# Input stage of a hybrid attention block: all eight token tiles first, or the first four and then the projections

## The chip, the cores and the metric

The kernel runs on one core of a Trainium2 chip. The metric is device time in microseconds (us): the median of three runs is 789.06 us (788.49 to 789.99). The profile is of one execution.

Engines: PE (TensorE, matmuls), DVE (VectorE), ACT (ScalarE), POOL (GpSimd), SP (SyncE, which issues most DMAs).

## The reference, cut to what matters

One decoder layer: an adaLN-modulated RMSNorm of `x`, one combined input projection, two attention groups, and an output projection with a residual and a final norm. All shapes are 1024 tokens by 1024 features, float32. The change touches only the first lines:

```python
mod = jax.nn.silu(c) @ ada_w[l] + ada_b[l]             # ada_w: 1024 x 3072
shift, scl, gate = jnp.split(mod, 3, axis=-1)
h = rms_norm(x, norm_g[l]) * (1.0 + scl[:, None, :]) + shift[:, None, :]
proj = h @ w_in[l]                                      # 1024 x 2744, split into 13 parts
(q_n, kc_n, vc_n, ks_n, vs_n, kw_n, vw_n, ...) = jnp.split(proj, IN_OFFSETS, axis=-1)
```

Everything after the first projections (compression, three sparse branches, latent attention, output) is the same in both kernels.

## The kernel before, in words

Tokens lie in eight tiles of 128 (`x_load(t)`, 512 KB each), features in eight blocks of 128 (index `k`). The input stage makes, for each block `k`, the modulated and transposed activations `h` of all 1024 tokens, split into a high part `hh[k]` and a low part `hl[k]` (both fp32r), and feeds them at once into two projections: `kc` (256 columns, features on the partitions, four PSUM banks `kcT{ci}_{hf}`, where `hf` is the token half) and `ks` (256 columns, tokens on the partitions, of tiles 0 to 3 only, two banks). Each product is three matmuls: high by high, high weight by low weight, low by high (`mm_kc` L315, `mm_ks` L325). All further projections (`pj`, L589) follow once `hh` and `hl` are complete.

A token tile passes `x_stat` (ACT squares and sums it, L351; DVE L164 and a POOL power L165 make its reciprocal norm), `x_turn` (DVE scales it, L356; PE transposes it in eight 128x128 pieces, L362) and `x_put` (ACT L370 and DVE L372 copy it out of PSUM into `xnT`).

A block's modulation needs two columns of `silu(c) @ ada_w`. `ad_load(k)` brings 1 MB in two halves, each of two DMAs. `mod_acc` adds the first six of eight row groups on DVE (L288, L290), the last two go to PE (L284), and `mod_mm` (L297) adds the sum over partitions; for block 0 all eight go to PE. `mod_cols` (DVE L302 to L305) makes scale and bias `ab`, `h_high` (ACT L310, twice) applies them, `h_low` (DVE L313) forms the low part. `w_split` splits the weights of two blocks at a time: ACT rounds (`whi`, L262), POOL subtracts (`wlo`, L263).

The order of the work in this stage is written out by hand for all five engines (`tc.manual_schedule`), so each engine executes its list in program order, and an instruction that waits holds back those behind it. First a loop over the eight tiles, with the modulation of block 0 between them; then a skewed loop over `s_`: in one step PE runs high products of block `s_-2`, the modulation of a later block and low products of block `s_-3`, while ACT and DVE prepare block `s_-1`. `x` tiles and `ada_w` halves share one ring of eight buffers (`big`). The sine and cosine tables (`tables`, DVE L396 to L416) and the copies of `kc` out of PSUM (`kc_evac`, DVE L442, ACT L444) close the stage.

Of the kernel before, what the change touches and what calls it, by code (L numbers as in the profile page):

```python
# [73 lines left out]
MLA_LAG = 3  # L74
MLA_WO = 27
AD_CUT = 2
MOD_CUT = 1
X_AD = 4
MOD_PE = (0,)
MOD_DVE = 6  # L80
MOD_FIRST = 4
TAB0 = 4
ACC0 = {5: ((0, 0, 2),), 6: ((0, 2, 4),), 7: ((0, 4, 6),), 8: ((0, 6, 8),), 9: ((1, 0, 2),)}
ENGS0 = ("PE", "SP", "DVE", "Activation", "Pool")
MLA_MIX = (40, 43)
WRING = 12
# [8 lines left out]
def f32(ap):  # L95
    return ap.bitcast(F32)
# [11 lines left out]
def hybrid_block(ctx, tc, x, c, positions, ada_w, ada_b, norm_g, w_in, cmp_pos, cmp_k_w1, cmp_k_w2,  # L108
# [148 lines left out]
    def w_split(k2, pl, tag, wmax, bufs, dst):  # L257
        raw = raws.pop((tag, k2))
        for j in range(2):
            whi = pl.tile([P, wmax], F32R, name="whi" + tag, tag="whi" + tag, bufs=bufs)  # L260
            wlo = pl.tile([P, wmax], F32R, name="wlo" + tag, tag="wlo" + tag, bufs=bufs)
            nc.scalar.activation(whi[:, :256], raw[:, j, :256], AF.Copy)  # L262
            nc.gpsimd.tensor_tensor(wlo[:, :256], raw[:, j, :256], f32(whi[:, :256]), op=ALU.subtract)  # L263
            dst[2 * k2 + j] = (whi, wlo)

    def ad_load(k):
        ads[k] = []
        for q in range(AD_CUT):
# [3 lines left out]
                nc.sync.dma_start(ad[:, :, j, :], ada_r[:, q * n:(q + 1) * n, o + k * P:o + (k + 1) * P])  # L272
            ads[k].append(ad)

    def mod_acc(k, k0, k1):
        if k0 == 0:
            pas[k] = mx_bank(f"mod{k}")
        first = 0 if k in MOD_PE else MOD_DVE
        n = KD // AD_CUT
        for kk in range(k0, k1):  # L280
            src = ads[k][kk // n][:, kk % n]
            if kk >= first:
                for j in range(2):
                    nc.tensor.matmul(pas[k][:, j:j + 1], src[:, j], sc[:, kk:kk + 1], start=(kk == first and j == 0),  # L284
                                     stop=(kk == KD - 1 and first == 0), skip_group_check=True)
            elif kk == 0:
# [12 lines left out]

    def mod_cols(k):  # L300
        pa = pas.pop(k)
# [145 lines left out]
    with tc.manual_schedule(engines={mybir.EngineType[e] for e in ENGS0}):  # L447
        nc.sync.dma_start(rows[0:8], c.rearrange("o (k p) -> (o k) p", p=P))
        x_load(0)
        small_loads()  # L450
        for t in range(1, X_AD):
            x_load(t)
        ad_load(0)
        for t in range(X_AD, NT):
            x_load(t)
        kc_raw(0)
        ks_raw(0)
        ad_load(1)
# [19 lines left out]
        def skew(k, i0, i1):
            for i in range(i0, i1):
                if k < KD:  # L480
                    mod_acc(k, 4 + i, 5 + i)
                if k + 1 < KD:
                    mod_acc(k + 1, i, i + 1)

        mod_mm(0)
        mod_cols(0)
        h_high(0)
        ks_split(0)
        mod_acc(1, 2, 4)
        for s_ in range(1, KD + 3):  # L490
            if s_ + 1 < KD:
                ad_load(s_ + 1)
            if s_ % 2 == 1 and s_ // 2 + 1 < KD // 2:
                kc_raw(s_ // 2 + 1)
                ks_raw(s_ // 2 + 1)
            if 1 < s_ < KD:
                (kc_split if s_ % 2 else ks_split)(s_ // 2)
            if MOD_FIRST <= s_ <= KD:
                mod_mm(s_ - 1)
            if 0 <= s_ - 2 < KD:  # L500
                mm_kc(s_ - 2, (0, 1))
            skew(s_, 0, MOD_CUT)
            if 1 < s_ <= KD:
                if s_ < MOD_FIRST:
                    mod_mm(s_ - 1)
                mod_cols(s_ - 1)
                h_high(s_ - 1)
            skew(s_, MOD_CUT, 4)
            if 2 < s_ < 6:
                next(post)  # L510
            if s_ == KD - 1:
                tables(TAB0)
            if s_ == KD:
                tables(9)
            if s_ - 1 < KD:
                h_low(s_ - 1)
            if 0 <= s_ - 2 < KD - 1:
                mm_ks(s_ - 2, (0, 1))
            if 0 <= s_ - 3 < KD:
                mm_kc(s_ - 3, (2,))  # L520
                if s_ - 3 == KD - 1:
                    mm_ks(s_ - 3, (0, 1))
                mm_ks(s_ - 3, (2,))
# [1072 lines left out]
```

## Time and profile before

| What | us |
|---|---|
| median of three runs | 789.06 |
| the profiled execution | 788.64 |
| its span (first to last instruction) | 786.9 |
| around the span | 1.74 |
| PE busy over the span | 739.3 |
| DVE busy | 583.6 |
| ACT busy | 396.3 |
| POOL busy | 228.0 |

Times inside the trace count from the start of the span. A matmul's end is modelled, so start-to-start distances say more than its duration. [...] The stage that the change touches is the first tenth of the span, up to the first `pj` matmul.

### The profile page before, as it was taken

How to read it: one execution, taken by the hardware profiler on the slowest of the kernel's cores; microseconds unless marked ns; L12 is line 12 of the kernel's file. 1: busy time of each engine (PE TensorE's matmuls, PEld its weight loads, DVE VectorE, ACT ScalarE, POOL GpSimd, SP SyncE). 2: the span in 40 equal slices, each digit the busy share in tenths (PEclk: the TensorE clock that was granted, in tenths of full speed). 3: DMA queues.
4: the chain of work that ended last, by engine and by line, in shares of the span. 5: the costliest groups of instructions: out<-in, count | busy, mean ns of one | idle time of the engine just before them, and what ended most of it. 6: DMA issues, size and time to landing. Idle time of an engine off the chain costs nothing.

```text
span 786.9 us, 17257 instructions
## 1 busy us (share of the span) xinstructions
PE 739.3 (94%) x6464; PEld 653.9 (83%) x6464; DVE 583.6 (74%) x1549; ACT 396.3 (50%) x697; POOL 228.0 (29%) x287
## 2 busy tenths in 40 slices
PE   4999999999999999997899999999988989999996
PEld 3988998989999999995677887777877777888885
DVE  3688745587688788888898889987888878654433
ACT  5354534133122331217899977987556566632212
POOL 3334433154231143504443312110200040154322
PEclk9599999999999999999999999999999979999999
DMA  8961423242531121103311123013010140435431
GB/s 307 262 197 49 127 55 108 61 121 80 162 95 48 44 52 47 36 31 97 93 47 44 43 56 82 22 57 80 10 28 16 52 151 29 151 131 185 144 113 54
DMA packets 60513, 70.18 MB, mean 89 GB/s; under 512 B 5957, under 2 KB 46728, under 8 KB 60430
## 3 DMA queue, kind: packets, MB, share of 16 engines
q1 hardware_dynamic: 55646, 64.62, 27.8%
q10 hardware_dynamic: 4784, 4.47, 1.7%
q8 instruction: 51, 0.84, 0.4%
q14 instruction: 32, 0.26, 0.1%
HBM read 48.33 MB, written 11.53 MB: 76 GB/s over the span
## 4 chain that ended last, share of the span: by engine, by line
PE 76%; DVE 9%; issue 4%; ACT 4%; DMA 4%; POOL 2%; SPq 1%; POOLq 0%; DVEq 0%; ACTq 0%
PE pj L589 24%; PE out L1528 11%; PE o L937 5%; PE pm L841 4%; PE s L994 3%; PE s L995 3%; PE kcT L321 2%; PE mo L937 2%; PE hid L642 2%; PE kq L1180 2%; PE ms L1301 2%; DVE L L1010 2%; PE ms L1302 2%; PE ms L1303 2%; PE mm L1256 2%
## 5 line engine op out<-in xcount | busy, mean ns | idle before, releaser
L589 PE MATMUL pj<-whi,hh 128*128 128x288 f32 (+2 forms) x544 | 161.4, 297 | 0.0
L589 PE MATMUL pj<-wlo,hh 128*128 128x288 f32 (+2 forms) x544 | 158.6, 292 | 0.0
L589 PE MATMUL pj<-whi,hl 128*128 128x288 f32 (+2 forms) x544 | 157.6, 290 | 0.0
L589 PEld LDWEIGHTS pj<-wlo,hh 128*128 128x128 f32 x544 | 102.5, 189 | 1.4
L589 PEld LDWEIGHTS pj<-whi,hh 128*128 128x128 f32 x544 | 102.5, 189 | 0.4
L589 PEld LDWEIGHTS pj<-whi,hl 128*128 128x128 f32 x544 | 102.2, 188 | 0.0
L1010 DVE TENSOR_TENSOR L<-E,H 128x1024 f16<-128x1024 f32 x74 | 92.0, 1243 | 13.1 <-ACT H L1005 11.4
L799 DVE CUSTOM_DVE_ANT_0 junk<-pm,maskw 128x256 bf16<-128x256 f32 (+3 forms) x160 | 77.7, 486 | 16.4 <-PE pm L841 4.4
L1004 ACT ACTIVATE E<-s 128x1024 f32<-128x1024 f32 x74 | 76.4, 1032 | 19.8 <-PE s L995 12.2
L937 PEld LDWEIGHTS <-H 128*128 128x128 f16 x1184 | 57.2, 97 | 30.2 <-issue 17.5
L968 POOL TENSOR_TENSOR mixn<-mixn,tmp 128x256 f32<-128x256 f32 x32 | 44.8, 1400 | 108.7 <-DVE tmp L967 101.9
L1005 ACT ACTIVATE H<-s 128x1024 f16<-128x1024 f32 x74 | 76.2, 1030 | 0.0
L841 PE MATMUL pm<-ka,qall 128*128 128x448 f32 (+5 forms) x208 | 67.2, 323 | 0.2 <-DVE mp L796 0.2
L937 PE MATMUL o<-v,H 128*128 128x65 f16 (+1 forms) x1056 | 60.0, 195 | 4.6 <-DVE mixn L964 4.6
L211 POOL TENSOR_TENSOR wlo<-wraw,whi 128x288 fp32r<-128x288 f32 (+2 forms) x64 | 51.7, 832 | 31.6 <-ACT whi L210 29.3
L994 PE MATMUL s<-qa,ka 128*128 128x512 f32 x132 | 57.9, 439 | 2.9 <-ACT H L1005 2.5
L937 PE MATMUL o<-v,L 128*128 128x65 f16 x528 | 56.7, 193 | 0.0
L937 PEld LDWEIGHTS <-L 128*128 128x128 f16 x592 | 55.7, 100 | 0.0
L708 ACT ACTIVATE zt<-pj 128x288 f32<-128x288 f32 (+1 forms) x32 | 12.2, 384 | 74.3 <-PE pj L589 62.6
L1314 ACT ACTIVATE lat<-ms 128x1024 f32<-128x1024 f32 (+2 forms) x40 | 32.6, 815 | 31.1 <-PE ms L1303 14.9
L1316 DVE TENSOR_TENSOR mL<-lat,mH 128x1024 f16<-128x1024 f32 (+2 forms) x40 | 39.0, 988 | 9.7 <-ACT mH L1315 9.5
L995 PE MATMUL s<-qall,kb_early 128*128 128x512 f32 x108 | 43.4, 401 | 0.0
(384 smaller groups left out, 1892.1 us busy)
## 6 DMA issues: line engine op xcount, KB each, us to landing
ad<-in_ada_w_dram SPq DMA_DIRECT2D x32, 256.0 KB
wraw<-in_w_in_dram SPq DMA_DIRECT2D x20, 288.0 KB
x<-in_x_dram SPq DMA_DIRECT2D x8, 512.0 KB
gw<-in_ada_w_dram SPq DMA_DIRECT2D x32, 128.0 KB
qa<-qall SPq DMA_DIRECT2D x32, 128.0 KB
wor<-in_w_out_dram SPq DMA_DIRECT2D x16, 256.0 KB
xr<-in_x_dram SPq DMA_DIRECT2D x8, 512.0 KB
out_dram<-y SPq DMA_DIRECT2D x7, 512.0 KB
```

Of the source, the lines that this page charges most:

```text
L211: split.tensor_tensor(wlo[:, :width], raw[:, j, :width], f32(whi[:, :width]), op=ALU.subtract)
L589: nc.tensor.matmul(pt[:, :width], a[k][:, ts], b[:, :width], start=(n == 0), stop=(n == 23))
L799: nc.vector.tensor_tensor_reduce(out=junk[:, :w], in0=scores, in1=mask, scale=1.0, scalar=2.0 * NEG, op0=ALU.add, op1=ALU.max, accum_out=dst)
L841: nc.tensor.matmul(bank[:, :total_w], lhs, keys, start=True, stop=True)
L937: nc.tensor.matmul(po[:, c0:c0 + hi - lo], a[:n, qs], v[:, lo:hi], start=start and j == 0, stop=stop and j == 2, skip_group_check=True)
L968: nc.gpsimd.tensor_tensor(mv, mv, tmp, op=ALU.add)
L994: nc.tensor.matmul(dst, a, staged[u], start=True, stop=False)
L995: nc.tensor.matmul(dst, b, qc[u], start=False, stop=mk is None)
L1004: nc.scalar.activation(Et, pS, AF.Exp, scale=SC_NSA)
L1005: nc.scalar.activation(ph, pS, AF.Exp, scale=SC_NSA)
L1010: nc.vector.tensor_tensor(pl, Et, ph, op=ALU.subtract)
L1528: nc.tensor.matmul(po, a[:, kk], b[hf][k][:, cs.start - hf * 512:cs.stop - hf * 512], start=(n == 0), stop=(n == 23))
```

## The change

The loop over tiles is cut at tile 4. Tiles 0 to 3 are loaded, normed and transposed as before; then a loop over blocks `k` makes modulation, `h` and both projections for the first 512 tokens. Tiles 4 to 7 are normed and transposed inside blocks 1 to 3 (`x_work`). The second token half of `h` and of `kc` (`second`) follows inside blocks 4 to 7 (`SECOND`). Block 0 now also adds six row groups on DVE. `h_high` and `h_low` work on 512 columns at a time, so there are twice as many of them; `tables` is spread over blocks 3 to 7. The loads are issued in the new order of use.

```diff
-ACC0 = {5: ((0, 0, 2),), 6: ((0, 2, 4),), 7: ((0, 4, 6),), 8: ((0, 6, 8),), 9: ((1, 0, 2),)}
+KC_RING = 6
+SECOND = {4: (0, 1), 5: (2, 3), 6: (4,), 7: (5, 6, 7)}
...
-    def h_high(k):
-        hfs[k] = sp.tile([P, S], F32, name=f"hf32_{k}", tag="hf32", bufs=2)
-        for dst in (hh[k], hfs[k]):
-            nc.scalar.activation(dst, xnT[:, k], AF.Identity, scale=ab[:, 0, k:k + 1], bias=ab[:, 1, k:k + 1])
+    def h_high(k, hf):
+        hs = slice(hf * 512, (hf + 1) * 512)
+        hfs[k, hf] = sp.tile([P, 512], F32, name=f"hf32_{k}_{hf}", tag="hf32", bufs=4)
+        for dst in (hh[k][:, hs], hfs[k, hf]):
+            nc.scalar.activation(dst, xnT[:, k, hs], AF.Identity, scale=ab[:, 0, k:k + 1], bias=ab[:, 1, k:k + 1])
...
-        for s_ in range(NT + 2):
-            if s_ < NT:
+        for s_ in range(6):
+            if s_ < 4:
                 x_stat(s_)
...
+        for t in (4, 5):
+            x_load(t)
+        ad_load(2)
+        kc_raw(1)
+        ks_raw(1)
+        kc_split(0)
+        ks_split(0)
+        mod_acc(0, 0, MOD_DVE)
...
+        def second(k, part):
+            if part == 0:
+                h_high(k, 1)
+            else:
+                h_low(k, 1)
+                mm_kc(k, 1, (0, 1, 2))
+
+        x_work = {1: ((x_stat, 4),), 1.5: ((x_turn, 4), (x_stat, 5)), 2: ((x_put, 4), (x_turn, 5), (x_stat, 6)),
+                  2.5: ((x_put, 5), (x_turn, 6), (x_stat, 7)), 3: ((x_put, 6),), 3.5: ((x_turn, 7), (x_put, 7))}
+        late_loads = {0: ((x_load, 6), (x_load, 7)), 1: ((ad_load, 3), (kc_raw, 2), (ks_raw, 2)),
+                      2.5: ((ad_load, 4), (ad_load, 5)), 3: ((kc_raw, 3), (ks_raw, 3)), 3.5: ((ad_load, 6), (ad_load, 7))}
...
+        for k in range(KD):
+            mod_acc(k + 1, 0, 2)
+            mod_mm(k)
+            mod_cols(k)
+            if k:
+                mm_kc(k - 1, 0, (2,))
+                mm_ks(k - 1, (2,))
+            h_high(k, 0)
+            if k % 2 and k < KD - 1:
+                kc_split(k // 2 + 1)
+                ks_split(k // 2 + 1)
+            extra(k)
...
+            mod_acc(k + 1, 2, MOD_DVE)
+            h_low(k, 0)
+            mm_kc(k, 0, (0, 1))
+            mm_ks(k, (0, 1))
...
+            for j in SECOND.get(k, ()):
+                second(j, 1)
+            extra(k + 0.5)
+            if k > 2:
+                tables(1)
```

Two places of the instruction lists matter, one on PE and one on DVE. In these rows the digit behind a name is its block or tile (`mod2` is block 2, `x4` tile 4), the number after the underscore only tells buffers apart.

PE before, between the high products of block 1 and the low products of block 0:

```order
L321 MATMUL kcT1_1_361<-hh1_91,wloa_310 128x512
L297 MATMUL mod2_391<-ones_pp_71,acc2_392 128x1 x2
L284 MATMUL mod3_426<-sc_77,ad3_1_406 128x1 x4
L329 MATMUL ks0_0_362<-whi_374,hh1_91 128x256
L329 MATMUL ks0_0_362<-wlo_375,hh1_91 128x256
```

PE of the changed kernel, from the end of block 1's high products to the start of block 2's:

```order
L323 MATMUL ks0_1_289<-wlo_276,hh1_91 128x256
L356 MATMUL xT4_0_400<-ident_66,x4_249 128x128 x4
L356 MATMUL xT4_1_405<-ident_66,x4_249 128x128 x4
L287 MATMUL mod2_418<-sc_77,ad2_1_256 128x1 x4
L291 MATMUL mod2_418<-ones_pp_71,acc2_327 128x1 x2
L315 MATMUL kcT0_0_286<-hl1_99,whia_267 128x512
L315 MATMUL kcT1_0_287<-hl1_99,whia_267 128x512
L323 MATMUL ks0_0_288<-whi_275,hl1_99 128x256 x2
L323 MATMUL ks0_1_289<-whi_275,hl1_99 128x256 x2
L356 MATMUL xT5_0_440<-ident_66,x5_251 128x128 x4
L356 MATMUL xT5_1_445<-ident_66,x5_251 128x128 x4
```

Tile 4's transposes now stand ahead of block 2's modulation, and tile 5's ahead of block 2's products; before, the products of two blocks and the modulation of a third were interleaved, and all transposes lay ahead of them.

DVE before, from block 1's columns to block 2's:

```order
L305 TENSOR_TENSOR ab_76<-mod1_354,cols_75 128x1
L290 SCALAR_TENSOR_TENSOR acc2_392<-ad2_1_383,sc_77,acc2_392 128x256
L290 SCALAR_TENSOR_TENSOR acc3_427<-ad3_0_403,sc_77,acc3_427 128x256 x3
L313 TENSOR_TENSOR hl1_99<-hf32_1_434,hh1_91 128x1024
L290 SCALAR_TENSOR_TENSOR acc3_427<-ad3_1_406,sc_77,acc3_427 128x256
L288 TENSOR_SCALAR acc4_482<-ad4_0_454,sc_77 128x256
L302 SCALAR_TENSOR_TENSOR sums_131<-mod2_391,cols_75 128x1
```

DVE of the changed kernel, from block 1's columns to block 2's:

```order
L298 TENSOR_TENSOR ab_76<-mod1_330,cols_75 128x1
L160 TENSOR_SCALAR rv_367<-ssx_129 128x1
L377 CAST pos_f_132<-pos_i_124 8x128
L378 CAST posc_134<-posc_i_125 64x1
L281 SCALAR_TENSOR_TENSOR acc2_327<-ad2_0_253,sc_77,acc2_327 128x256 x2
L281 SCALAR_TENSOR_TENSOR acc2_327<-ad2_1_256,sc_77,acc2_327 128x256 x2
L308 TENSOR_TENSOR hl1_99<-hf32_1_0_346,hh1_91 128x512
L350 TENSOR_SCALAR x4_249<-x4_249,rsx_130 128x1024
L160 TENSOR_SCALAR rv_412<-ssx_129 128x1
L279 TENSOR_SCALAR acc3_415<-ad3_0_370,sc_77 128x256
L281 SCALAR_TENSOR_TENSOR acc3_415<-ad3_0_370,sc_77,acc3_415 128x256
L295 SCALAR_TENSOR_TENSOR sums_131<-mod2_418,cols_75 128x1
```

The statistic `rv` of tile 4, which needs ACT's square, now stands ahead of block 2's accumulations, of `hl1` and of the scaling of tile 4. On ACT that square stands behind block 1's two `h` instructions (`hh1`, `hf32_1_0`) and four weight conversions (`whia`, `whi` of blocks 2 and 3); on POOL the four subtractions of the same weights stand ahead of tile 4's power `rsx`.

## Rows read from the trace of the kernel before

**Rows 1.** Chain of waits in time order: start us, us, what (xcount).

```profile
31.97 0.17 DVE sums L302
...
32.49 1.25 ACT hh L310
33.78 3.78 PE kcT L321 x8
37.56 0.65 PE mod L297 x4
...
39.91 1.92 PE ks L329 x8
...
66.18 1.98 PE kcT L321 x8
...
68.95 1.05 PE ks L329 x8
...
71.75 1.96 PE kcT L321 x8
...
81.68 7.98 PE pj L589 x67
```

**Rows 2.** Windows: stretch, length, busy PE, PEld, DVE, ACT, POOL (xcount), PEclk, DMA, GB/s.

```profile
33.78:42.60 8.82, 8.82 (x31) 7.85 (x32) 8.03 (x17) 5.00 (x9) 4.15 (x4) 0.50 0.86 255
42.60:81.50 38.90, 38.13 (x240) 33.84 (x239) 33.68 (x77) 19.16 (x28) 15.19 (x15) 1.00 0.42 122
...
125.00:126.00 1.00, 0.34 (x2) 0.34 (x3) 0.94 (x7) 0.76 (x2) 0.67 (x1) 1.00 0.69 218
...
128.00:129.00 1.00, 1.00 (x6) 0.97 (x5) 1.00 (x3) 0.98 (x2) 0.00 (x0) 0.50 0.10 23
...
131.00:132.00 1.00, 1.00 (x6) 0.95 (x5) 0.00 (x0) 0.00 (x0) 0.00 (x0) 0.79 0.73 220
...
73.40:75.50 2.10, 2.10 (x15) 1.87 (x14) 2.06 (x10) 1.94 (x2) 0.00 (x0) 1.00 0.08 16
```

**Rows 3.** Timeline of DVE: start us, us, line, operation, out<-in [idle before <-releaser].

```profile
13.42 0.69 DVE L372 COPY xnT<-xT 128x512 f32<-128x512 f32 x1
16.16 0.15 DVE L164 TENSOR_SCALAR rv<-ssx 128x1 f32<-128x1 f32 x1 [2.05 <-ACT sq L351]
16.25 0.75 DVE L356 TENSOR_SCALAR x<-x,rsx 128x1024 f32<-128x1024 f32 x1
...
36.20 1.75 DVE L313 TENSOR_TENSOR hl<-hf,hh 128x1024 fp32r<-128x1024 f32 x1
...
45.40 1.91 DVE L290 SCALAR_TENSOR_TENSOR acc<-ad,sc,acc 128x256 f32<-128x256 f32 x4
...
68.89 1.09 DVE L414 TENSOR_TENSOR ang<-inv,posT 128x384 f32<-128x384 f32 x1
...
71.99 1.21 DVE L313 TENSOR_TENSOR hl<-hf,hh 128x1024 fp32r<-128x1024 f32 x1
...
79.59 3.48 DVE L442 COPY lat<-kcT 64x256 f32<-64x256 f32 x8 [2.39 <-PE kcT L321]
```

**Rows 4.** Timeline of POOL, same columns.

```profile
12.69 1.01 POOL L165 TENSOR_TENSOR rsx<-rv,mhalf 128x1 f32<-128x1 f32 x1 [0.93 <-DVE rv L164]
...
20.69 1.41 POOL L263 TENSOR_TENSOR wloa<-wrawa,whia 128x256 fp32r<-128x256 f32 x2
...
35.24 4.15 POOL L263 TENSOR_TENSOR wlo<-wraw,whi 128x256 fp32r<-128x256 f32 x4 [12.03 <-ACT whi L262]
```

**Rows 5.** Timeline of PE at the transposes of one tile.

```profile
18.67 1.85 PE L362 MATMUL xT<-ident,x 128*128 128x128 f32 x8 [0.46 <-DVE x L356]
```

**Rows 6.** Timeline of ACT, same columns.

```profile
11.28 1.05 ACT L351 ACTIVATE sq<-x 128x1024 bf16<-128x1024 f32 x1
...
47.80 0.71 ACT L262 ACTIVATE whi<-wraw 128x256 fp32r<-128x256 f32 x2
```

**Rows 7.** Timeline of SP: an `ada_w` block's four DMA issues.

```profile
21.05 3.73 SPq L272 DMA_DIRECT2D ad<-in_ada_w_dram  x4
```

More of the change, by code (lines that the diff above doesn't have):

```diff
@@ L76 @@
 AD_CUT = 2
-MOD_CUT = 1
-X_AD = 4
-MOD_PE = (0,)
 MOD_DVE = 6
-MOD_FIRST = 4
-TAB0 = 4
-ACC0 = {5: ((0, 0, 2),), 6: ((0, 2, 4),), 7: ((0, 4, 6),), 8: ((0, 6, 8),), 9: ((1, 0, 2),)}
+KC_RING = 6
+SECOND = {4: (0, 1), 5: (2, 3), 6: (4,), 7: (5, 6, 7)}
 ENGS0 = ("PE", "SP", "DVE", "Activation", "Pool")
@@ L273, in ad_load, with ad_part @@
             ads[k].append(ad)
+    def ad_part(k, kk):
+        return ads[k][kk // (KD // AD_CUT)][:, kk % (KD // AD_CUT)]
     def mod_acc(k, k0, k1):
[L276 to L286, printed above, removed]
+        for kk in range(k0, k1 if k < KD else k0):
+            src = ad_part(k, kk)
+            if kk == 0:
                 accs[k] = sp.tile([P, 2, P], F32, name=f"acc{k}", tag="acc", bufs=2)
@@ L292, in mod_mm @@
     def mod_mm(k):
-        if k in MOD_PE:
-            return
+        pa = pas[k] = mx_bank(f"mod{k}")
+        for kk in range(MOD_DVE, KD):
+            for j in range(2):
+                nc.tensor.matmul(pa[:, j:j + 1], ad_part(k, kk)[:, j], sc[:, kk:kk + 1],
+                                 start=(kk == MOD_DVE and j == 0), stop=False, skip_group_check=True)
         acc = accs.pop(k)
         for j in range(2):
-            nc.tensor.matmul(pas[k][:, j:j + 1], acc[:, j, :], ones_pp[:, 0:1], start=False, stop=True,
-                             skip_group_check=True)
+            nc.tensor.matmul(pa[:, j:j + 1], acc[:, j, :], ones_pp[:, 0:1], start=False, stop=True, skip_group_check=True)
     def mod_cols(k):
@@ L305, in mod_cols, with h_low, mm_kc @@
         nc.vector.tensor_tensor(ab[:, 1, k:k + 1], pa[:, 1:2], cols[:, 8 + k:9 + k], op=ALU.add)
-    def h_high(k):
-        hfs[k] = sp.tile([P, S], F32, name=f"hf32_{k}", tag="hf32", bufs=2)
-        for dst in (hh[k], hfs[k]):
-            nc.scalar.activation(dst, xnT[:, k], AF.Identity, scale=ab[:, 0, k:k + 1], bias=ab[:, 1, k:k + 1])
-    def h_low(k):
-        nc.vector.tensor_tensor(hl[k], hfs.pop(k), f32(hh[k]), op=ALU.subtract)
-    def mm_kc(k, ns):
+    def h_high(k, hf):
[3 more added lines that the diff above has]
+            nc.scalar.activation(dst, xnT[:, k, hs], AF.Identity, scale=ab[:, 0, k:k + 1], bias=ab[:, 1, k:k + 1])
+    def h_low(k, hf):
+        hs = slice(hf * 512, (hf + 1) * 512)
+        nc.vector.tensor_tensor(hl[k][:, hs], hfs.pop((k, hf)), f32(hh[k][:, hs]), op=ALU.subtract)
+    def mm_kc(k, hf, ns):
         whi, wlo = wkc[k]
@@ L319, in mm_kc @@
                 for ci in range(2):
-                    for hf in range(2):
-                        nc.tensor.matmul(pkc[ci][hf], a[:, ci * P:(ci + 1) * P], b[k][:, hf * 512:(hf + 1) * 512],
-                                         start=(k == 0 and n == 0), stop=(k == KD - 1 and n == 2))
+                    nc.tensor.matmul(pkc[ci][hf], a[:, ci * P:(ci + 1) * P], b[k][:, hf * 512:(hf + 1) * 512],
+                                     start=(k == 0 and n == 0), stop=(k == KD - 1 and n == 2))
     def mm_ks(k, ns):
@@ L339, in kc_split @@
     def kc_split(k2):
-        w_split(k2, sp, "a", 256, 4, wkc)
+        w_split(k2, sp, "a", 256, KC_RING, wkc)
     def ks_split(k2):
@@ L450, in hybrid_block @@
         small_loads()
-        for t in range(1, X_AD):
+        for t in range(1, 4):
             x_load(t)
         ad_load(0)
-        for t in range(X_AD, NT):
-            x_load(t)
         kc_raw(0)
@@ L462, in hybrid_block @@
         nc.vector.tensor_copy(cols, pr[:, :64])
-        for s_ in range(NT + 2):
-            if s_ < NT:
+        for s_ in range(6):
+            if s_ < 4:
                 x_stat(s_)
-            if 1 <= s_ <= NT:
+            if 1 <= s_ <= 4:
                 x_turn(s_ - 1)
@@ L469, in hybrid_block @@
                 x_put(s_ - 2)
-            for k, a, b in ACC0.get(s_, ()):
-                mod_acc(k, a, b)
             if s_ == 1:
                 nc.scalar.activation(sc, cols[:, 0:8], AF.Silu)
-            if s_ == 6:
-                kc_split(0)
-        pkc = [[mm_bank("kcT0_0"), mm_bank("kcT0_1")], [mm_bank("kcT1_0"), mx_bank("kcT1_1")]]
-        pks = [o_bank(f"ks0_{i}", i) for i in range(2)]
[L478 to L509, printed above, removed]
-                next(post)
[L511 to L523, printed above, removed]
@@ new lines, in hybrid_block @@
+        for t in (4, 5):
[6 more added lines that the diff above has]
+        mod_acc(0, 0, MOD_DVE)
+        pkc = [[mm_bank("kcT0_0"), None], [mm_bank("kcT1_0"), None]]
+        pks = [o_bank(f"ks0_{i}", i) for i in range(2)]
+        def second(k, part):
[6 more added lines that the diff above has]
+                  2.5: ((x_put, 5), (x_turn, 6), (x_stat, 7)), 3: ((x_put, 6),), 3.5: ((x_turn, 7), (x_put, 7))}
@@ new lines, in hybrid_block, with extra @@
+        late_loads = {0: ((x_load, 6), (x_load, 7)), 1: ((ad_load, 3), (kc_raw, 2), (ks_raw, 2)),
+                      2.5: ((ad_load, 4), (ad_load, 5)), 3: ((kc_raw, 3), (ks_raw, 3)), 3.5: ((ad_load, 6), (ad_load, 7))}
+        def extra(at):
+            for f, i in x_work.get(at, ()) + late_loads.get(at, ()):
+                f(i)
+        for k in range(KD):
[10 more added lines that the diff above has]
+            extra(k)
+            if k == 4:
+                pkc[0][1], pkc[1][1] = mm_bank("kcT0_1"), mx_bank("kcT1_1")
+            for j in SECOND.get(k, ()):
+                second(j, 0)
+            if 1 <= k <= 3:
+                next(post)
+            mod_acc(k + 1, 2, MOD_DVE)
+            h_low(k, 0)
+            mm_kc(k, 0, (0, 1))
+            mm_ks(k, (0, 1))
+            if k == KD - 1:
+                mm_kc(k, 0, (2,))
+                mm_ks(k, (2,))
+            for j in SECOND.get(k, ()):
+                second(j, 1)
+            extra(k + 0.5)
+            if k > 2:
+                tables(1)
@@ L524, in hybrid_block @@
+        tables(9)
         start.close()
```

## The prediction

> **What bounds the kernel now.** I read the chain of waits first, in order of time. The reader is to see PE's first `kcT` matmul at 33.78, its first `pj` matmul at 81.68, and PE holding nearly all of the chain between; two neighbouring blocks start at 66.18 and 71.75, so a block costs PE 5.57, and eight make 44.6 of the 47.9 [rows 1]. The stage is bound by PE once it runs. [...] Third, the timelines of DVE, POOL and ACT for the price of each step. One row shows how such a list holds work back: DVE's statistic `rv` at 16.16 sat 2.05 waiting for ACT's square, and the scaling of tile 3 ran behind it at 16.25 [rows 3], though POOL had that tile's power ready at 12.69 + 1.01 = 13.70 [rows 4].
>
> **The earlier start.** Tile 3 is now turned behind the copy of 13.42 + 0.69 = 14.1, so to 14.9. Its eight transposes cost 1.85 at the low clock [rows 5], half that at the high one; I take 1.1, then a copy of 0.69: 16.7. Six accumulations of block 0 follow on DVE, at 1.91/4 = 0.48 each [rows 3]: 2.8. Beside them POOL runs four weight subtractions (4.15 for four with DVE busy [rows 4]), and a DVE instruction with two inputs was 1.75 instead of 1.21 beside such work [rows 3], 0.54 more; three of the six pay it: 1.6. With two accumulations of block 1 (0.85, as the order has it) that is 21.9. The columns take 32.49 - 31.97 = 0.52 up to `h` [rows 1]. `h` on 512 columns isn't in the trace: between 0.62 (half of 1.25 [rows 1]) and 1.25. Two 256-column conversions are 0.71 [rows 6], so I take 0.70. First projections at 23.1 instead of 33.8: a lead of 10.7. Of PE's own work, block 0's modulation loses ten of sixteen matmuls, ahead of that point and hidden by DVE's longer sum.
>
> [...]
>
> **What PE has to do from there.** A half block is one block less half its `kc`: 5.57 - 1.48 = 4.1 at the high clock, of which high products 0.99 + 1.05 = 2.05 (`kcT` 1.98 for eight, `ks` 1.05 [rows 1]), modulation 1.2, low products 0.95. At the low clock: 1.89 + 1.92 = 3.8, 39.91 - 37.56 = 2.35, 1.9 [rows 1]. A second half costs 1.48. New beside them are 32 transposes, 0.9 to 1.1 per tile.
>
> **The waits that come.** I walk the lists, block by block.
>
> Block 0, low clock: high products 23.1 to 26.9, block 1's modulation to 29.2, low products to 31.1. Block 1's `h` is ready at 29.2 + 0.52 + 0.70 = 30.4, in time. The clock rose 8.8 after the first projection before [rows 2]; I let it rise at 32. Block 1's high products end at 33.4, and PE comes to tile 4's transposes.
>
> Tile 4 is not there. ACT has from 29.7 on two `h` instructions (1.3), four conversions (1.4) and the square (1.05 [rows 6], and I take 0.2 to read its sum): 33.7. POOL's first subtraction starts at 31.4, four cost 4.15, the power 1.01: 36.6. DVE waits for the square until 33.7; behind that wait are two casts, block 2's four accumulations (1.91 and one slowed, 0.54), `hl1` (0.65) and the scaling (0.75). Transposes at 38.0: PE idles 4.6.
>
> Block 2: transposes to 39.1, and after such a wait the low clock. In the stretch at 125 PE was busy 0.34 of a microsecond, at 128 the clock was 0.50, and it came back within 131 to 132 [rows 2]. So modulation to 41.5, columns 42.0, copy and scaling of tile 5 43.4, transposes 45.2, high products to 47.6 with the clock rising again. DVE's next statistic needs ACT's two `h`, a copy and a square, 3.2 after 42.0; then four accumulations, `hl2`, a copy (0.69) and a scaling, 4.0: tile 6 at 49.2, PE idle 1.6.
>
> Block 3: tile 6 to 50.2, modulation 51.4, `h` 52.6, high products 54.7. DVE after its columns (51.9): copy, four accumulations beside POOL (2.45), `hl3`, scaling: tile 7 at 56.5, PE idle 1.8; transposes 57.5, modulation 58.7. Now DVE has the copy, `ang` (1.09 [rows 3]) and two accumulations ahead of block 4's columns: 60.1, 60.6, `h` 61.3; PE's low products end at 59.6, idle 1.7.
>
> Blocks 4 to 7: 4 x 4.1 + 8 x 1.48 = 28.2. Between a block's modulation and its `h` (0.52 + 0.70) lie only 0.95 of low products, 0.3 four times; twice second-half `h` instructions and weight conversions hold ACT up, 0.5 together. PE ends at 91.1.
>
> The bank: `pj` needs a PSUM bank that the copies of `kcT` free. Before, these began at 79.59 [rows 3], two before `pj`. Now they stand on DVE behind the last low part (88.7: eight `h` instructions of 0.7 are ACT's tail), the table steps (the same ones and two columns steps are 2.06 [rows 2]) and four memsets (I take 0.9): 91.6. Two copies of 3.48/8 = 0.43 and two of ACT's as long: 93.3.
>
> The loads I cost at nothing. `ad` of block 4, which stands ahead of block 3's columns on DVE, can be issued in full once PE has done block 2's modulation, 41.5; four issues take 3.73 [rows 7], so it lands about 45.5, and is wanted at 49.3. If that cover of 4 went, each microsecond more would go straight to the end. SP's other new waits are on steps of two blocks earlier.
>
> **The sum.** 93.3 - 81.7 = 11.6 later; what follows is one PE stream that starts at `pj`, so I carry it to the end. The profiled execution took 788.64 (span 786.9 and 1.74 around it), 0.42 below the median of the runs; with 11.6 it is 800.2, the median 800.7. I say 800.
>
> Bounds. Short: DVE never slowed (-2.5), POOL's subtractions as alone, 1.41 for two [rows 4] (-1.3), the high clock from block 0's second microsecond on (-3) and no second low stretch (-1.5), the copies of `kcT` in time (-2.2): +1 if all came, 789.5. Long: the clock falls at each wait, below.
>
> **Rivals.**
>
> The waits are shorter than walked: about half of the short list comes true. For it: POOL's 1.41 was measured with DVE hardly beside it, so the pair may cost less in a different overlap. Against: DVE is at 33.7 of 38.9 already. The loss is then 4 to 7: 794.
>
> The clock falls at every wait. For it: the microsecond at 125, in which PE was busy 0.34, was followed by more than 3 us at 0.50 from 128 on, though PE was busy again throughout [rows 2]. Three more such stretches (tile 6, tile 7, block 4), of about 3.5, cost half of each: 5.3, so 805.5. Against: the walk's waits there are 1.6 to 1.8, and part of the slow time falls into other waits of PE. So I put it behind the walk. [...]
>
> PE is never short of work: faster. The mechanism is tile 4's scaling, ready when block 1's high products end; it decides at 33.4, where my walk has 38.0. If tiles 4 to 7 were always in time, PE would need 8 x 5.57 - 1.2 for block 0's modulation, 4.0 of transposes, and 4.4 for 8.8 at the low clock: 23.1 + 43.4 + 4.0 + 4.4 = 74.9 instead of 81.7, 782. For it: the lead of 10.7 is safe. Against: the row at 16.16, where the same two instructions stood in the same order and the second waited.
>
> No change: lead and waits cancel, as the short bound nearly has it.
>
> **Chances.** The walk 0.54 (796 to 804), shorter waits 0.19 (791 to 796), the clock 0.15 (804 to 808), PE never short 0.07, no change 0.05. A difference of 0.2% (1.6) is about what a measurement of this kernel can tell from none: faster 0.07, same 0.05, slower 0.88. Range 791 to 807, which leaves out the last two cases and the top of the clock's; the walk's own is 796 to 804.
>
> **What the profile would show.** First `kcT` near 23; PE idle 3 to 5 ahead of tile 4's transposes, released by DVE's scaling; DVE's `rv` waiting for ACT's square; a second stretch at 0.50 near 40; block 4 near 61; `pj` near 93, released by a copy of `kcT`. I am wrong if PE goes through blocks 1 to 3 without those waits, if the first `kcT` comes after 27, if the loads end the waits, or if the delay at `pj` shrinks later in the kernel.

## The result, and the profile after

The changed kernel takes 809.5 us (median of 4 runs, 807.7 to 811.6) against 788.8 (4 runs, 788.0 to 790.0): 1.025 times the time before, interval 1.021 to 1.030. Forecast were 800, with 791 to 807 as the range. The profiled execution took 811.57, span 809.8, so 22.9 more than the span before. Times here and below are of fast runs; one run of one kernel below (812.5, modulation 0) was slow and is left out.

To see where they arise, take three marks that both programs have: the first `pj` matmul, the first of the 280 columns wide ones some 12 us later, and the first `hid` matmul (of the compression, which follows). They stood at 81.52, 93.54 and 125.66, and stand at 98.60, 113.37 and 145.49: 17.1, 19.8 and 19.8 later. The rest, 3.1, comes between 561 and 682 of the kernel before.

The windows of the changed kernel come first (stretch, length, busy PE, PEld, DVE, ACT, POOL, then PEclk, the granted TensorE clock as a share of full speed, DMA share, GB/s; the sum line adds up the busy times). They answer to [rows 2].

```profile
0.00:24.27 24.27, 8.89 (x46) 8.17 (x46) 12.88 (x30) 10.54 (x21) 7.53 (x16) 0.90 0.91 286
24.27:50.00 25.73, 22.05 (x88) 19.60 (x89) 13.16 (x36) 10.26 (x19) 5.47 (x8) 0.57 0.65 204
50.00:60.50 10.50, 7.81 (x61) 7.18 (x60) 7.06 (x14) 3.83 (x8) 4.26 (x5) 0.99 0.88 250
60.50:66.40 5.90, 5.90 (x21) 5.03 (x22) 4.56 (x14) 4.34 (x6) 0.00 (x0) 0.50 0.12 40
...
98.50:104.50 6.00, 5.90 (x27) 5.91 (x28) 3.42 (x17) 5.22 (x20) 0.46 (x1) 0.50 0.49 145
...
sum 145.49, PE 116.61 PEld 106.96 DVE 84.66 ACT 66.33 POOL 44.41; mean PE 16.66 PEld 15.28 DVE 12.09 ACT 9.48 POOL 6.34
```

Two more windows of the kernel before, cut at its first `kcT` and at `hid`:

```profile
0.00:33.78 33.78, 22.05 (x105) 20.66 (x106) 15.05 (x37) 16.89 (x31) 9.76 (x18) 0.78 0.90 291
33.78:125.66 91.88, 89.78 (x614) 84.30 (x615) 69.32 (x184) 45.02 (x103) 40.01 (x52) 0.95 0.40 115
```

Up to `hid` PE was busy 22.05 + 89.78 = 111.8 and idle 13.8. Now it is busy 116.6 and idle 145.49 - 116.61 = 28.9. So of the 19.8, 15.0 are idle time and 4.8 more busy time. And the first `kcT` starts 9.5 earlier (24.27 for 33.78), but by that point PE has been busy for 8.89 in place of 22.05, 13.2 less. Some of that work went to DVE (ten matmuls of block 0's modulation); the rest, above all the transposes of four tiles, now stands behind the start.

Now PE's timeline of the changed kernel, at the places that the prediction walked (start, length, instruction, and in brackets the idle time ahead with its releaser):

```profile
38.77 1.06 PE L356 MATMUL xT<-ident,x 128*128 128x128 f32 x8 [3.04 <-DVE rv L160]
...
44.64 1.97 PE L356 MATMUL xT<-ident,x 128*128 128x128 f32 x8 [0.63 <-ACT xnT L364]
...
50.21 1.04 PE L356 MATMUL xT<-ident,x 128*128 128x128 f32 x8
...
58.35 1.06 PE L356 MATMUL xT<-ident,x 128*128 128x128 f32 x8 [2.37 <-DVE x L350]
...
62.76 1.22 PE L315 MATMUL kcT<-hh,whia 128*128 128x512 f32 x2
...
95.06 0.63 PE L315 MATMUL kcT<-hl,whia 128*128 128x512 f32 x2
98.60 0.58 PE L587 MATMUL pj<-whi,hh 128*128 128x256 f32 x1 [2.91 <-ACT lat L438]
...
104.31 0.41 PE L587 MATMUL pj<-whi,hl 128*128 128x256 f32 x1
104.52 0.36 PE L587 MATMUL pj<-whi,hh 128*128 128x256 f32 x1
104.72 0.29 PE L587 MATMUL pj<-wlo,hh 128*128 128x256 f32 x1
104.84 0.28 PE L587 MATMUL pj<-whi,hl 128*128 128x256 f32 x1
```

The four tiles are the `xT` rows. Tiles 4 and 7 are waited for at length (3.04 and 2.37), tile 5 for 0.63, tile 6 not at all, and behind the waits for tile 7 (2.37) and `pj` (2.91) stand the windows at 0.50: 60.5 to 66.4, and 98.5 to 104.5. There `pj` matmuls start 0.21 apart (104.31, 104.52), then 0.12 (104.72, 104.84). The 28 that start 0.21 apart cost 14.77 - 12.02 = 2.75 between the first `pj` and the first wide one.

DVE and ACT, ahead of the first `h`, of tile 4 and of `pj`, answer to [rows 3, 6]:

```profile
22.08 0.48 DVE L281 SCALAR_TENSOR_TENSOR acc<-ad,sc,acc 128x256 f32<-128x256 f32 x1
22.88 0.16 DVE L295 SCALAR_TENSOR_TENSOR sums<-mod,cols 128x1 f32<-128x1 f32 x1 [0.32 <-PE mod L291]
...
34.71 0.15 DVE L160 TENSOR_SCALAR rv<-ssx 128x1 f32<-128x1 f32 x1 [3.85 <-ACT sq L345]
...
34.98 2.38 DVE L281 SCALAR_TENSOR_TENSOR acc<-ad,sc,acc 128x256 f32<-128x256 f32 x4
37.28 0.68 DVE L308 TENSOR_TENSOR hl<-hf,hh 128x512 fp32r<-128x512 f32 x1
37.88 0.75 DVE L350 TENSOR_SCALAR x<-x,rsx 128x1024 f32<-128x1024 f32 x1
...
95.60 0.27 DVE L616 MEMSET vc<- 128x258 f16 x1
...
96.77 2.60 DVE L436 COPY lat<-kcT 64x256 f32<-64x256 f32 x6
```

The same of ACT:

```profile
23.40 0.81 ACT L304 ACTIVATE hh<-xnT,ab 128x512 fp32r<-128x512 f32 x1 [5.29 <-DVE ab L298]
...
32.32 0.70 ACT L258 ACTIVATE whia<-wrawa 128x256 fp32r<-128x256 f32 x2
32.93 0.71 ACT L258 ACTIVATE whi<-wraw 128x256 fp32r<-128x256 f32 x2
33.54 1.04 ACT L345 ACTIVATE sq<-x 128x1024 bf16<-128x1024 f32 x1
...
97.77 1.59 ACT L438 ACTIVATE lat<-kcT 64x256 f32<-64x256 f32 x4 [4.46 <-issue]
```

DVE's sums end at 22.56, and the columns wait 0.32 more for PE. Later DVE sits 3.85 at tile 4's statistic until ACT, behind four weight conversions, has squared it. Four accumulations and `hl` follow, and only then the scaling at 37.88. At the end the last `kcT` is done near 95.7, but its copies begin at 96.77, behind table steps and memsets.

### The profile page after: what moved, and what is told of

Its sections match the earlier page's. It is cut to its first block, busy times and chain, and to the rows that moved or that the text cites. A ratio compares the mean times of both kernels' runs of the same rounds, so it can differ in the third digit from the quotient of the medians.

```text
span 809.8 us, 17243 instructions
## 1 busy us (share of the span) xinstructions
PE 745.6 (92%) x6444; PEld 655.9 (81%) x6444; DVE 585.1 (72%) x1563; ACT 400.7 (49%) x713; POOL 222.5 (27%) x287
## 4 chain that ended last, share of the span: by engine, by line
PE 69%; DVE 8%; issue 4%; ACT 4%; DMA 2%; POOL 1%; SPq 0%; POOLq 0%; DVEq 0%; ACTq 0%
PE pj L587 24%; PE out L1526 11%; PE o L935 5%; PE pm L839 4%; PE s L992 3%; PE s L993 3%; PE mo L935 2%; PE ms L1299 2%; PE hid L640 2%; PE kq L1178 2%; PE ms L1300 2%; PE ms L1301 2%; PE mm L1254 2%; PE qr L1223 1%; DVE L L1008 1%
```

## The experiments

All times in us; the marks are those of each kernel's one profiled execution, the time is the median of its runs. "Last kcT" is the start of the last two such matmuls. `hid` is the mark at which the stage's delay is complete. "Late" is what the stretch from the first scores of the second attention (561 before) to the output projection (682) added against the first profile of the kernel before.

| kernel | first kcT | last kcT | hid | hid later by | late | time, median (range) |
|---|---|---|---|---|---|---|
| before | 33.78 | 79.62 | 125.66 | 0 | 0 | 788.8 (788.0 to 790.0) |
| before, again | 33.75 | 79.59 | 125.63 | 0.0 | 2.8 | 789.3 (785.7 to 791.9) |
| changed | 24.27 | 95.06 | 145.49 | 19.8 | 3.1 | 809.5 (807.7 to 811.6) |
| bank | 23.69 | 95.55 | 140.58 | 14.9 | 3.9 | 810.0 (808.7 to 811.0) |
| pj's wait filled | 24.51 | 94.81 | 142.56 | 16.9 | 1.5 | 808.5 (807.0 to 811.2) |
| front filled | 24.71 | 95.44 | 145.70 | 20.0 | 2.8 | 809.3 (806.5 to 810.8) |
| tile 7's wait filled | 24.35 | 93.60 | 142.62 | 17.0 | 3.2 | 809.1 (808.6 to 809.8) |
| earlier statistics | 23.19 | 87.72 | 136.78 | 11.1 | 1.0 | 801.6 (800.0 to 806.1) |
| modulation 0 on PE | 22.77 | 92.40 | 141.66 | 16.0 | 4.3 | 807.7 (800.1 to 810.2) |
| three edits | 22.46 | 85.82 | 130.90 | 5.2 | 2.2 | 795.6 (794.6 to 797.3) |
| modulation ahead | 21.88 | 92.86 | 137.58 | 11.9 | -0.5 | 801.6 (799.8 to 805.0) |
| tables late | 22.32 | 85.43 | 129.96 | 4.3 | 4.3 | 796.0 (791.3 to 797.3) |

**A free bank for `pj`.**

```diff
-pkc[0][1], pkc[1][1] = mm_bank("kcT0_1"), mx_bank("kcT1_1")
+pkc[0][1], pkc[1][1] = mx_bank("kcT0_1"), mx_bank("kcT1_1")
```

> The changed kernel with one edit: both second-half accumulators of kcT take banks of the ring that the modulation uses, so that a bank of the projections' ring is free when pj begins. In the changed kernel PE idles 2.91 ahead of pj (98.60) and then runs 28 pj matmuls at 0.214 in place of 0.119. Theory A (the wait for the bank costs itself and sets the clock back, 2.9 + 2.7): pj begins near 95.7 with no idle time, its first matmuls are 0.12 apart, and the kernel is 5 to 6 faster than the changed one, 804. Theory B (pj would be late anyway, by the copies of kcT or by its weights): pj still begins after 97 or waits at its second tile, and the gain is under 1.5.

`hid` comes 4.9 earlier than in the changed kernel, near what theory A has: with a bank free, 23 `pj` matmuls run among the `kcT` ones from 66.43 on. The kernel's time, which theory A put at 804, shows nothing of it (810.0). In its profile all but 0.6 of the 4.9 is gone by the end: 2.0 went between 167 and 190 of the kernel before, 1.4 more up to 402, and 0.8 in the late stretch, beside the changed kernel. PE's timeline there:

```profile
97.25 0.39 PE L587 MATMUL pj<-whi,hh 128*128 128x256 f32 x1 [0.95 <-ACT lat L438]
97.47 0.28 PE L587 MATMUL pj<-wlo,hh 128*128 128x256 f32 x1
...
187.50 0.44 PE L688 MATMUL qT<-ident,qt 128*128 128x128 f32 x2 [2.36 <-POOL qt L172]
...
188.29 0.42 PE L587 MATMUL pj<-whi,hh 128*128 128x256 f32 x1
188.51 0.41 PE L587 MATMUL pj<-wlo,hh 128*128 128x256 f32 x1
```

Behind the wait of 0.95 ahead of `pj` the matmuls are 0.12 apart from the second on. At 187.50 a wait of 2.36 for POOL, 1.75 in the kernel before, is followed by matmuls 0.22 apart, with the clock at 0.69 from 187.5 to 193. Whether the bank's edit brings this wait about is open: the three kernels below that hold the same bank (three edits, modulation ahead, tables late) lose nothing there. In the other two stretches the unchanged kernel moves by 1.1 and 2.8 from its first profile to its second (below).

**`pj`'s wait filled.** The matmuls stand behind the last `kcT` and write a bank that nobody reads.

```diff
+junk = mx_bank("junk")
+for i in range(20):
+    nc.tensor.matmul(junk[:, :256], hh[0][:, :P], hh[0][:, :256], start=True, stop=True)
 tables(9)
```

> The changed kernel with 20 matmuls of 256 columns, whose result nobody reads, in the wait ahead of pj (20 x 0.119 = 2.4 of the 2.9 idle). Nothing that pj waits for is moved. Theory A (the idle time is what puts the clock down): pj begins at 98.5 as before, but its first 28 matmuls are 0.12 apart: 2.7 faster than the changed kernel, some 807. Theory B (the clock falls for another reason, such as the rate of the kcT matmuls just before): the first pj matmuls stay 0.21 apart and the time is the changed kernel's.

PE's timeline of this kernel, from the last `kcT` on:

```profile
95.28 2.54 PE L523 MATMUL junk<-hh 128*128 128x256 f32 x20
98.32 0.39 PE L590 MATMUL pj<-whi,hh 128*128 128x256 f32 x1 [0.50 <-ACT lat L438]
98.54 0.28 PE L590 MATMUL pj<-wlo,hh 128*128 128x256 f32 x1
98.66 0.29 PE L590 MATMUL pj<-whi,hl 128*128 128x256 f32 x1
```

`pj` starts where it did (98.32), and its matmuls are 0.12 apart from the second on. `hid` is 2.9 earlier. That is what theory A has, but one profile doesn't show that the filling did it: with the same wait of 2.91 left as it was, the kernel with tile 7's wait filled (below) has no slow `pj` matmuls either. The time, 808.5, lies within the changed kernel's runs.

**The front filled**: 20 such matmuls ahead of the last part of block 0's modulation, and 14 ahead of tile 4 (`junk` issues n of them).

```diff
+        if k == 0:
+            junk(10, wks[0][0][:, :P], wks[0][0][:, :256])
+            junk(10, wks[1][0][:, :P], wks[1][0][:, :256])
...
+            if at == 1.5:
+                junk(14, hh[0][:, :P], hh[0][:, :256])
```

> The changed kernel with matmuls of 256 columns, whose result nobody reads, in two waits of PE: 20 ahead of the last part of block 0's modulation (PE idles 4.4 there) and 14 ahead of tile 4's transposes (3.0). Lists of the other engines are as they were. Theory clock (the low clock until 50 is what makes the stage long): the clock rises before 35, kcT's last matmul ends 6 to 9 earlier than 95.6, and the kernel takes 801 to 804. Theory waits (the lists of DVE, ACT and POOL set the pace, PE waits instead of running slowly): the clock rises early as well, but PE's idle time grows by about as much, and the last kcT is within 2 of 95.6.

Its windows in the front:

```profile
24.00:30.00 6.00, 5.29 (x21) 4.91 (x22) 2.94 (x7) 1.36 (x2) 0.00 (x0) 0.50 1.09 385
30.00:36.00 6.00, 6.00 (x32) 5.53 (x33) 1.20 (x8) 4.64 (x9) 2.77 (x4) 0.70 0.71 211
```

Tile 4's transposes start 14.43 behind the first `kcT` (39.14), as against 14.50 in the changed kernel, and the last `kcT` 70.73 behind it, as against 70.79. But the filling hardly tested the front's speed: the clock was at 0.50 from 24 to 30 all the same, and `ks` matmuls were 0.12 apart, not 0.21, only from 33.95 on. Three other profiles test it. Bank, `pj`'s wait filled and tile 7's wait filled have the changed kernel's lists up to tile 4 and fill nothing ahead of it. The clock from 30 to 36 was 0.96 with `pj`'s wait filled, and from 20.2 to 40.3 it was 0.7 or more with tile 7's wait filled; the changed kernel has 0.50 and 0.58 there. Here is a window of the changed kernel (its tile 4 is the row of 38.77 above), then the same window and tile 4's row of `pj`'s wait filled:

```profile
30.00:36.00 6.00, 5.73 (x20) 4.85 (x20) 1.64 (x8) 4.93 (x10) 3.21 (x5) 0.50 0.59 175
```

```profile
30.00:36.00 6.00, 2.98 (x18) 2.35 (x16) 2.05 (x8) 4.94 (x10) 3.81 (x5) 0.96 0.92 279
...
38.16 1.94 PE L356 MATMUL xT<-ident,x 128*128 128x128 f32 x8 [4.86 <-DVE rv L160]
```

In these three profiles tile 4 came 13.2 to 13.7 behind the first `kcT`, 0.8 to 1.3 earlier, and in the one of the row PE waited 4.86 for it in place of 3.04. Of that lead nothing was left at block 4: 38.7 behind the first `kcT` with the bank and with `pj`'s wait filled, 38.5 in the changed kernel. Up to there PE's speed in the front did not set the pace: it stood the more idle. The clock theory falls for this stretch by these profiles, not by the edit.

**Tile 7's wait filled** with 18 such matmuls, placed ahead of tile 7's transposes like the 14 above.

> The changed kernel with 18 matmuls of 256 columns, whose result nobody reads, in PE's wait for tile 7 (18 x 0.119 = 2.1 of 2.37 idle at 58.35). Theory clock: the granted clock stays up in 60.7 to 66.3, where it was 0.50, the last kcT comes 2 to 2.9 earlier than 95.06 and so does pj. Theory waits: the clock stays up too, but block 4's h and the second halves' h on ACT are no earlier, PE idles instead, and the last kcT is within 1 of 95.06.

PE's timeline, at tile 7 and at block 4:

```profile
57.48 1.06 PE L356 MATMUL xT<-ident,x 128*128 128x128 f32 x8 [0.25 <-DVE x L350]
...
61.89 1.22 PE L315 MATMUL kcT<-hh,whia 128*128 128x512 f32 x2 [1.06 <-ACT hh L304]
```

Nearer to the theory of waits: it took 69.25 from the first `kcT` to the last in place of 70.79, but of these 1.5 the transposes of tile 7 were already 1.0 earlier (33.1 behind the first `kcT`, 34.1 in the changed kernel), in a profile whose clock was higher in the front (0.7 or more from 20.2 to 40.3, 0.58 in the changed kernel). From tile 7's transposes to the last `kcT` it took 36.12 in place of 36.71, 0.6 won. A new wait of 1.06 for block 4's `h` stands behind them, and there the clock fell after all (0.69 from 63.0 to 66.4): the two `kcT` matmuls of 61.89 take 1.22, and the `ks` ones behind them are 0.21 apart up to 64.8. The slow stretch is shorter (to 65.0, not 66.3), not gone. The rest of the 2.9 at `hid` came behind `pj`, where nothing was filled. The same wait of 2.91 stands there, and the clock was 1.00 behind it (a row of PE, then a window):

```profile
97.13 0.39 PE L591 MATMUL pj<-whi,hh 128*128 128x256 f32 x1 [2.91 <-ACT lat L438]
```

```profile
97.00:103.00 6.00, 5.87 (x49) 5.87 (x50) 3.40 (x18) 5.26 (x20) 0.46 (x1) 1.00 0.48 144
```

The time, 809.1, is the changed kernel's.

**Earlier statistics** for tiles 4 to 7; the tiles are also turned half a block earlier, and a block's work on tiles now stands ahead of its weight conversions.

```diff
+x_work = {0: ((x_sq, 4), (x_sq, 5)), 0.5: ((x_rv, 4), (x_rv, 5)), 1: ((x_turn, 4), (x_sq, 6), (x_sq, 7)),
+          1.5: ((x_put, 4), (x_rv, 6), (x_rv, 7), (x_turn, 5)), 2: ((x_put, 5), (x_turn, 6)), 2.5: ((x_put, 6),),
+          3: ((x_turn, 7),), 3.5: ((x_put, 7),)}
...
+extra(k)
 if k % 2 and k < KD - 1:
     kc_split(k // 2 + 1)
     ks_split(k // 2 + 1)
-extra(k)
```

> The changed kernel with the statistics of tiles 4 to 7 issued one block earlier, ahead of the weight conversions on ACT and behind the accumulations on DVE, and the turns of tiles 4 to 7 half a block earlier. Same work. Theory waits (the place of the statistics in the in-order lists makes PE wait for tiles 4 and 7: 3.0 + 2.4, and what the clock loses after): no idle time of PE ahead of the transposes, the clock rises before 40, pj at 88 to 92, the kernel 6 to 10 faster than the changed one: 800 to 804. [...]

PE's timeline, at tiles 4 and 6 and at block 4:

```profile
31.04 1.89 PE L363 MATMUL xT<-ident,x 128*128 128x128 f32 x8
...
40.20 1.97 PE L363 MATMUL xT<-ident,x 128*128 128x128 f32 x8 [1.49 <-ACT xnT L371]
...
55.90 0.73 PE L315 MATMUL kcT<-hh,whia 128*128 128x512 f32 x2 [1.88 <-ACT hh L304]
```

The theory of waits holds: 64.5 from the first `kcT` to the last in place of 70.8, `hid` 8.7 earlier, and 7.9 off the time, the one single edit that the time shows. Which of its three moves did most isn't separated. Tile 4 (31.04) has no wait left; 0.54, 1.49 and 1.88 stand at tiles 5 and 6 and at block 4.

**Block 0's modulation on PE alone.**

```diff
-mod_acc(0, 0, MOD_DVE)
...
+first = MOD_DVE if k else 0
+for kk in range(first, KD):
```

> The changed kernel with block 0's modulation on PE alone (16 one-column matmuls in place of four, no sum on DVE), as it was in the kernel before. In the changed kernel DVE spends 17.34 to 21.8 on that sum and the first kcT follows at 24.27. Theory waits (the lists' places for tiles 4 to 7 set the pace, the start does not): the first kcT comes near 20, but PE waits longer for tile 4, whose square stands behind block 1's h on ACT; pj comes 1 to 3 earlier than 98.6 and the kernel takes 806 to 808.5. Theory lead (a lead at the start is kept in full): pj comes 4 earlier, 805.

The first `kcT` came at 22.77, not near 20: 32 one-column matmuls took PE 4.4 (so measured in the three edits' profile), little less than DVE's sum. `pj` is 2.7 earlier, `hid` 3.8. The time (807.7, runs from 800 to 810) settles nothing.

**The three edits**, then two attempts at more: the modulation of block k+1 ahead of half of block k's high products, and later table steps with tiles 5 and 6 turned later. Both of these add up three of block 0's eight modulation steps on DVE and the rest on PE.

> The three edits together: block 0's modulation on PE, the statistics of tiles 4 to 7 one block earlier, and the bank for pj. Theory waits: pj's place was 91.2 with the earlier statistics alone; the bank takes 2.9 off and the clock behind it 2.7, the modulation 3 to 4: the hid matmuls near 127 to 129 (125.66 before, 145.49 in the changed kernel), the kernel 791 to 795. Rival (another engine becomes the bound once those are gone, DVE or ACT with 5 to 5.5 a block): hid at 131 to 134, 797 to 800. For a version faster than the kernel before, hid would have to come below 125.

> An attempt at a version that beats both: the token halves, the earlier statistics and the bank as in the three edits together, block 0's modulation split (three of eight steps on DVE, the rest on PE), the modulation of block k+1 between the two groups of high products of block k on PE, so that its columns and h lie beside 1.05 + 0.95 of PE's work, and the table steps from block 4 on. In the three edits together PE still idled 1.8, 1.5 and 1.9 ahead of tile 5, tile 6 and block 4, and the clock fell behind the last for 6. Theory order (each of these is a place in a list): no wait over 1 between the first kcT (22) and the last, no low clock after 30, hid at 120 to 125, the kernel 783 to 790. Rival engine bound (DVE at 5.5 a block is the pace in the first four blocks, whatever the order): hid at 127 to 131, 792 to 796.

> A second attempt at a version that beats both, with the loop as changed: earlier statistics, the bank, three of eight modulation steps of block 0 on DVE, tile 5 turned at block 2 and tile 6 half a block later than in the three edits together, and the table steps from block 4 on, two each. It aims at the waits that were left there: 1.8 ahead of tile 5, 1.5 ahead of tile 6, 1.9 ahead of block 4 with 6 of low clock behind it. Theory order: these go, hid at 124 to 127 (130.9 with the three edits), 788 to 792. Rival engine bound: the idle time shows up elsewhere, hid at 130 or later, 795 or more.

```diff
+            mm_kc(k, 0, (0, 1))
+            if k < KD - 1:
+                mod_mm(k + 1)
+                mod_cols(k + 1)
+                h_high(k + 1, 0)
+            mm_ks(k, (0, 1))
```

```diff
+1.5: ((x_put, 4), (x_rv, 6), (x_rv, 7)), 2: ((x_turn, 5),), 2.5: ((x_put, 5), (x_turn, 6)), 3: ((x_put, 6), (x_turn, 7))
...
-            if k > 2:
-                tables(1)
+            if k > 3:
+                tables(2)
```

The three edits bring 795.6, 1.008 of the kernel before (1.006 to 1.011): 14 of the 21 lost are won back. The windows of that profile, cut at its first `kcT` and at `hid`:

```profile
0.00:22.46 22.46, 11.17 (x65) 10.53 (x65) 9.50 (x24) 10.54 (x21) 7.36 (x16) 0.93 0.86 277
22.46:130.90 108.44, 97.45 (x654) 89.15 (x654) 73.02 (x204) 55.83 (x129) 37.58 (x54) 0.95 0.43 130
```

One row of PE in it, tile 6:

```profile
38.36 1.09 PE L366 MATMUL xT<-ident,x 128*128 128x128 f32 x8 [1.50 <-ACT xnT L374]
```

PE is busy 108.6, less than before (111.8), and idle 22.3 against 13.8. The later tables come to the same (796.0; busy 107.5, idle 22.4), which is where their rival had them (`hid` at 129.96, 130 or later forecast). With the modulation ahead, weight conversions stand ahead of a tile's copy on ACT, and PE waits for DVE's sums (3.34 at 79.63): 801.6, slower than either theory had it. No order tried beats the kernel before, and between `order` and `engine bound` the runs don't decide: each list that was mended left idle time at other places.

**The kernel before, again.**

> The kernel before, unchanged, for a second profile. In five profiles of changed kernels the stretch from the first small-score matmuls (561 in the profile before) to the output projection (682) took 1.0 to 3.9 longer than in the profile before. If that is an effect of the change, this profile has the output projection at 681 to 683, as the first. If it is chance of the clock in that stretch, it lies elsewhere by 1 to 3 in this one.

Windows of the late stretch, the kernel before first, then its second profile:

```profile
630.00:650.00 20.00, 16.78 (x137) 14.12 (x136) 15.58 (x30) 13.10 (x20) 7.97 (x6) 0.74 0.42 144
650.00:682.00 32.00, 30.50 (x414) 26.74 (x413) 24.33 (x51) 22.40 (x31) 0.00 (x0) 1.00 0.14 40
```

```profile
630.00:650.00 20.00, 15.20 (x122) 12.15 (x123) 15.72 (x30) 11.72 (x18) 7.70 (x5) 0.76 0.35 120
650.00:683.00 33.00, 32.16 (x411) 27.93 (x410) 23.62 (x50) 22.18 (x30) 0.00 (x0) 0.94 0.12 37
```

The same program took 2.8 more there the second time, with the clock at 0.94 in place of 1.00 in its second part, and 1.4 less between `hid` and 402. So the 3.1 of the changed kernel's profile in this stretch are no effect that can be put down to the change.

## Why the prediction was wrong in size

The direction and the mechanism were right: the lead is lost again to waits of PE for tiles that stand late in the lists of DVE and ACT. From the first `kcT` to block 4's the walk had 38.2, and it took 62.76 - 24.27 = 38.5; that the two agree so well is luck in part, as PE waited less there than the walk's named waits (6.4, not 9.7) and ran longer at the low clock. The sum up to `hid` was 8.2 short (11.6, measured 19.8), in five terms (0.2 besides is the mark: the prediction took `pj` before from the chain, at 81.68, and its first matmul starts at 81.52):

- The lead, 10.7. Measured 9.5 (24.27, not 23.1): DVE's sums ended at 22.56, not 21.9, the columns waited 0.32 more for PE, and `h` on 512 columns took 0.81, not 0.70. 1.2 short.
- Tile 4, "PE idles 4.6", transposes at 38.0. Measured 3.04, at 38.77, released by DVE behind ACT's square, as walked; with `pj`'s wait filled, and the clock at 0.96 from 30 to 36, the same wait was 4.86. POOL was no part of it: four subtractions took 3.3, not 4.15. Tile 6 wasn't waited for (1.6 forecast), tile 7 was for 2.37 (1.8). The low clock, forecast up to 32 and then from 39 to 46, was there for most of the time up to 50 (0.57 from 24.27 on); but of a faster front nothing is left at block 4. Together 0.3 short. Earlier statistics removed 6.3 between the first `kcT` and the last: these waits are the largest single cause of the loss that an edit shows, and the walk had them nearly right.
- "Blocks 4 to 7: 4 x 4.1 + 8 x 1.48 = 28.2", with 1.7 for waits. This step failed: it took 32.9 from block 4's first `kcT` to the last one's end, 3.1 more. Its first 3.6 lie in the stretch at 0.50 behind tile 7's wait, which I put at half of that, 1.8 (an estimate: eight `kcT` took 3.78 at 0.50 and 1.98 at 1.00 [rows 1, 2]), and PE's waits from block 4 to the last `kcT` came to 2.9 in place of 1.7, 1.35 of it ahead of block 6.
- The bank, 2.2. Measured 2.9: 0.7 short.
- "What follows is one PE stream that starts at `pj`, so I carry it to the end." This step failed too: the stream began with matmuls 0.21 apart in place of 0.12, which took 2.75 more up to the first wide matmul. That the wait ahead of it is the cause is likely, not shown: its price ran from nothing to 2.75 in five profiles (below).

Behind `hid` the delay was carried, within 0.8, up to 561. The loads, which the walk cost at nothing, did cost nothing: between the first `kcT` and `pj` the profile has no wait of PE or DVE for a DMA.

So what came nearest wasn't the walk but the rival "The clock falls at every wait". It gave 5.3 for three more slow stretches and 805.5; there were two, 1.8 behind tile 7 and 2.75 behind `pj`, where it had none. I had held against it that waits of 1.6 to 1.8 are short and that slow time falls into other waits. The second was true of the front, up to block 4. The first did not hold: the waits came to 2.4 and 2.9, and with tile 7's filled even one of 1.06 had matmuls 0.21 apart behind it. The clock was at 0.50 behind tile 7's wait (60.5 to 66.4) and `pj`'s (98.5 to 104.5), but not behind every wait of that length (below).

The rival "PE is never short" asked for tile 4 at 33.4. With the earlier statistics tile 4 is there at 31.04, and the kernel is still slower: its mechanism was one wait of several. How little there was to win is in the two windows of the kernel before: ahead of its first `kcT` PE was busy for 22.05 of 33.78, most of it on work that has to be done anyway, and idle for 11.7; behind it, up to `hid`, it was idle for 2.1. The changed kernel has 15.4 and 13.5.

## What to carry to other kernels

Before a start is moved forward, see what the bounding engine does in the time to be gained: if it is busy there, the lead is paid back later, and only its idle time can be won (here the lead of 9.5 came with 13.2 less of PE's work done). Price a wait of PE by its length and by the slow matmuls behind it, also at the seam to the next stage; the second part is a range (nothing to 2.75 behind one wait here). Filling a wait with matmuls that nobody reads asks whether the slow clock costs anything, but one profile of it doesn't answer: the clock of one list differs from profile to profile (here 0.50 and 0.96 from 30 to 36), so set the filled profile beside several unfilled ones.

## What the runs showed of the hardware that was not expected

The same wait of 2.90 to 2.91 ahead of `pj` had different prices. From the first `pj` to the first wide one it takes 12.02 without a wait, and behind it 14.77 (changed), 13.60 (modulation 0), 13.42 (statistics), 13.31 (front filled) and 12.51 (tile 7 filled): 0.5 to 2.75 more. In the last of these the clock stayed at 1.00 from 97 to 103, so the slow matmuls behind one wait cost from nothing to 2.75.

Two waits of one length ended differently: behind 1.49 ahead of tile 6 the eight transposes took 1.97 (earlier statistics), behind 1.50 ahead of the same tile 1.09 (three edits).

In the front filled, 20 matmuls of 256 columns took 2.65 from 18.66 on, 0.13 each, and after two waits of 1.37 and 1.42, with four small matmuls between, the clock was at 0.50 in the window from 24 to 30. ScalarE took 0.81 for 512 columns, where 1024 had taken 1.25 [rows 1]: half the columns took two thirds of the time.
